# Two transformer layers on one core: the activation tile H, and all that is allocated behind it, 32 bytes further on in SBUF

## The chip, the cores and the metric

The kernel runs on one core of one Trainium2 chip. The time is device microseconds (us) of one execution. Three executions of the kernel before took 2331.41, 2332.02 and 2332.15 us; the median is 2332.02 us.

## What is computed

A sequence of 256 tokens with 2048 features, all in float32, goes through two layers. Layer 0 mixes tokens with gated linear attention, layer 1 with grouped-query attention. Both have the same MLP and the same gated embedding behind it. Cut to what matters here:

```python
for i in range(2):
    u = rms_norm(h, g_pre_mix[i])
    mix = gla_mixer(u, ...) if i == 0 else gqa_mixer(u, ...)        # both end with  o @ w_out
    h = h + rms_norm(mix, g_post_mix[i])
    hid = relu(rms_norm(h, g_pre_mlp[i]) @ w_mlp_up[i])              # [256, 2048] @ [2048, 8192]
    h = h + rms_norm((hid * hid) @ w_mlp_down[i], g_post_mlp[i])     # [256, 8192] @ [8192, 2048]
    gate = sigmoid(h @ w_ple_gate[i])                                # [256, 2048] @ [2048, 2048]
    h = h + rms_norm(gate * (p[i] @ w_ple_proj[i]), g_ple[i])
```

## The kernel before

**Three products for one.** Each float32 operand is split into a high and a low float32r part, and a product is made of three matmuls: high by high, high by low, low by high. Weights come by DMA in chunks of two contraction tiles by 512 columns (`raw`, 4 buffers), and ScalarE and VectorE split each into `whi` and `wlo` (4 buffers each, lines 91 and 92). An activation tile holds both parts beside each other: `X` and `H` are each 128 partitions by 16 contraction tiles by 512, where the first 256 elements of a contraction tile are the high part of the 256 tokens and the other 256 the low part.

**Two kinds of product.** `gemm_b` (lines 367 and 372) makes a transposed result: the weights are loaded into the array (they are the stationary operand, 128x128) and the activations stream through (the moving operand). A pair of its matmuls streams 512 and then 256 columns. `gemm_a` (lines 294 to 296) makes a result by rows: the activations are stationary and 512 columns of the weights stream. `gemm_out` (lines 333 to 335) is a `gemm_a` whose last 512 columns are made one row tile after the other, and for them half of the weights wait in the activation tile that is free at that time (`keep`). So in the gate's product `g` some matmuls stream weights out of `H` while `X` is stationary, and in the last down product `d` some stream weights out of `X` while `H` is stationary. The second row tile of these columns is made in two parts of 256 columns. In the profile a matmul is written out<-moving,stationary: `d<-whi,H` streams `whi` against a stationary piece of `H`.

**The order.** The stages follow one another on TensorE, in an order that is written out: q, k, v, then the output gate `og` and the output product `go` of layer 0; four times an up product `u` of 2048 columns (from `X` into `H`) and a down product `d` (from `H`); the gate product `g`; then in layer 1 `kp`, `vp`, `q`, the attention, the output product `ao`, and again four times `u` and `d`, and `g`. `H` is the stationary operand of `go`, `ao` and `d`; `X` that of `v`, `kp`, `vp`, `q` and `g`.

**Where the tiles lie.** Tile pools are laid out one behind the other, and every tile starts at a multiple of 32 bytes of each partition. By the built program `X` starts at byte 33,824, the `raw` buffers at 66,592 and every 4,096 bytes on, `whi` at 82,976 and `wlo` at 99,360 and every 4,096 bytes on: all of them 32 modulo 64. Their places also agree modulo 512, 1024 and 2048. `H` is the first tile of the pool `L1` (line 804) and starts at byte 171,968, which is 0 modulo 64. Matmul operands are pieces of 512, 1024 or 2048 bytes at multiples of 512 bytes within their tile, so each piece has its tile's place modulo 64. Behind `H` lie the other tiles of `L1` (the helpers `t1` and `t2` of the up product, `PT`, the gain rows, the low parts of keys and values `kvlow`) and, last, the attention's small pool `att`.

Of the kernel before, what the change touches and what calls it, by code (L numbers as in the profile page):

```python
# [10 lines left out]
F32 = mybir.dt.float32  # L11
# [6 lines left out]
P = 128  # L18
# [37 lines left out]


class WeightStream:
    """Weight chunks in the order of use: DMA in, split exactly into two float32r parts."""

    def __init__(self, nc, pool, nraw, nsplit):
        self.nc, self.pool, self.nraw, self.nsplit = nc, pool, nraw, nsplit
# [29 lines left out]
        self.todo.append(lambda: self.nc.vector.tensor_sub(lo, raw, hi.bitcast(F32)))  # L92

    def parts(self, i):
        """The first chunk comes one contraction tile at a time, so that PE starts early."""
        kt = self.chunks[i][1]
        return [(k, k + 1) for k in range(kt)] if i == 0 else [(0, kt)]

# [52 lines left out]
def kernel(ctx, tc, a, out):  # L151
# [9 lines left out]
    def acc(name):  # L161
        return psa.tile([P, 512], F32, tag="acc", name=name)
# [79 lines left out]
    def rstd_of(ss, dim, name):  # L242
        n = ss.shape[1]
        ms = sm.tile([P, 2], F32, tag="ms", name=name + "_ms")[:, :n]
        nc.vector.tensor_reduce(ms, ss, axis=AX.X, op=ALU.add)
        nc.vector.tensor_scalar(ms, ms, 1.0 / dim, EPS, op0=ALU.mult, op1=ALU.add)
        r = sm.tile([P, 2], F32, tag="rstd", name=name, bufs=3)[:, :n]
        nc.gpsimd.tensor_tensor(r, ms, mhalf[:, :n], op=ALU.pow)
        return r
# [24 lines left out]
    def region_open():  # L274
        region.enter_context(tc.manual_schedule(engines={mybir.EngineType.Activation, mybir.EngineType.DVE}))

    def gemm_a(op, ngroups, evac, nk=16, name="a", pair=False):
        nch = nk // KC
        order = [(g, c) for g in range(ngroups) for c in range(nch)]
        if pair:  # L280
            order = pair_order(nch) + [(g, c) for g in range(2, ngroups) for c in range(nch)]
        ps = {}
        for g, c in order:
            if c == 0:
                ps[g] = [acc(f"{name}_{g}_{t}") for t in range(NT)]
            hi, lo = W.get()
            seq = [(k, t) for k in range(KC) for t in range(NT)]
            if c == nch - 1:
                seq = [(k, t) for t in range(NT) for k in range(KC)]
            for k, t in seq:  # L290
                K = c * KC + k
                xh = op[:, K, t * P:(t + 1) * P]
                xl = op[:, K, T + t * P:T + (t + 1) * P]
                mm(ps[g][t], xh, hi[:, k], start=K == 0, stop=False)  # L294
                mm(ps[g][t], xh, lo[:, k], start=False, stop=False)  # L295
                mm(ps[g][t], xl, hi[:, k], start=False, stop=K == nk - 1)  # L296
                if K == nk - 1:
                    evac(g, t, ps[g][t])
            yield (g, c)

    def gemm_out(op, keep, evac, name, pair=False):
        """Four column groups; the last one row tile after the other, half of its weights waiting in `keep`."""
        nch = KT // KC
        p0 = W.pos + 3 * nch
        for c in range(NSPLIT):
            W.dest[p0 + c] = [keep[:, 4 * c + 2 * z:4 * c + 2 * z + 2].rearrange("p k n -> p (k n)") for z in range(2)]
        yield from gemm_a(op, 3, evac, name=name, pair=pair)
        for t in range(NT):
            parts = [(0, 512)] if t == 0 else [(0, 256), (256, 256)]
            ps = [acc(f"{name}_3_{t}_{o}") for o, _ in parts]  # L310
            order = [[c] for c in range(nch)]
            if t:
                order = order[NSPLIT:] + order[:NSPLIT]
                order[-2:] = [order[-2] + order[-1]]
            for n, cs in enumerate(order):
                end = n == len(order) - 1
                if t and end:
                    region_open()
                wt = {}
                for c in cs:  # L320
                    W.ahead()
                    wt[c] = W.pop(p0 + c) if t else W.split[p0 + c]
                if t and end:
                    W.pos += nch
                for (o, w), p_ in zip(parts, ps):
                    s = slice(o, o + w)
                    ck = [(c, k) for c in cs for k in range(KC)]
                    for c, k in ck:
                        K = c * KC + k
                        hi, lo = wt[c]  # L330
                        xh = op[:, K, t * P:(t + 1) * P]
                        xl = op[:, K, T + t * P:T + (t + 1) * P]
                        mm(p_[:, :w], xh, hi[:, k, s], start=n == 0 and k == 0, stop=False)
                        mm(p_[:, :w], xh, lo[:, k, s], start=False, stop=False)
                        mm(p_[:, :w], xl, hi[:, k, s], start=False, stop=end and (c, k) == ck[-1])
                    if end:
                        evac(3, t, p_[:, :w], o, w)
                yield (3, cs[0])
# [8 lines left out]
        return r  # L347

    def early(m, ss, name):
        """The update of the residual's first rows, while PE is at the second."""  # L350
        r = rstd_of(ss[:, :1, :4], D, name)
        for n in range(4):
            residual_n(m, r, n, (0,))
# [84 lines left out]
                                           op0=ALU.mult, op1=ALU.add)  # L438

    def boundary(m, ss, gain0, name, fill=(), late=None):  # L440
        """The normalised update of the residual and the next operand; fill: products that keep PE busy."""
        rstd = last_rstd(ss, name)
        mults = list(pend)
        pend.clear()
        W.ahead(1, lows=False)
        for f in fill[:-1]:
            f()()
        for o in (0, 256):
            nc.vector.scalar_tensor_tensor(h[:, 1, o:o + 256], m(1, 0)[:, o:o + 256], rstd, h[:, 1, o:o + 256],
                                           op0=ALU.mult, op1=ALU.add)  # L450
        W.lows()
        make_X(0, gain0)
        if late is not None:
            late(0)
        if fill:
            fill[-1]()()
        residual_n(m, rstd, 1, (1,))
        W.ahead(1)

        def hook(n):  # L460
            def f():
                make_X(n, gain0)
                if n == 2:
                    for g in mults:
                        g()
                if n < 3:
                    residual_n(m, rstd, n + 1, (1,))
                if late is not None:
                    late(n)
                if n == 3:  # L470
                    region.close()
            return f
        hooks = {0: [hook(1)], 2: [hook(2)], 4: [hook(3)]}
        if late is not None:
            at(hooks, 6, lambda: late(4))
        return hooks
# [137 lines left out]
    with tc.tile_pool(name="core", bufs=1) as cp:  # L614
# [150 lines left out]
        s = fold(ps, "lr", 32)  # L765
# [35 lines left out]
        sl = drive(gemm_a(X, 4, v_evac, name="v"), plan, sl)  # L801

    L1 = ctx.enter_context(tc.tile_pool(name="L1", bufs=1))
    H = L1.tile([P, KT, 512], F32R, name="H")

    def load_PT(i):
        pts = L1.tile([P, 2, T], F32, tag="pts", name=f"pts{i}")
        nc.scalar.dma_start(pts, a["pT"][i])
        PT = L1.tile([P, 2, 512], F32R, tag="PT", name=f"PT{i}")
        split_into(PT[:, :, :T], PT[:, :, T:], pts)  # L810
        return PT

    def og_evac(i, ps):
        s = fold(ps, f"og{i}")
        t1 = L1.tile([P, T], F32, tag="t1", name=f"og1_{i}", bufs=2)
        nc.vector.tensor_mul(t1, s, R0["r"])
        sg = L1.tile([P, T], F32, tag="t2", name=f"og2_{i}", bufs=2)
        nc.scalar.activation(sg, t1, AF.Sigmoid)
        nc.vector.tensor_mul(t1, t1, on[i // 4][:, i % 4])
        nc.vector.tensor_mul(t1, t1, sg)  # L820
        split_into(H[:, i, :T], H[:, i, T:], t1)
    drive(gemm_b(X, 4, og_evac, name="og"), plan, sl)
# [3 lines left out]
    mg = {}  # L826
    gr = gain_row(L1, a["g_post_mix"][0], "gpm0")
    ss = sm.tile([P, NT, 5], F32, tag="ss", name="ssm0")
    drive(gemm_out(H, X, out_evac(mg, gr, ss, "go"), "go"))

    RM = {}
# [13 lines left out]
    def mlp_ple(i, hooks, PT):  # L845
# [5 lines left out]
        def up_evac(f, ps):  # L851
# [3 lines left out]
            nc.scalar.activation(s2, s, AF.Square)  # L855
            split_into(H[:, f, :T], H[:, f, T:], s2)

# [16 lines left out]
        for q in range(4):  # L874
# [3 lines left out]
            if q < 3:  # L878
                drive(gemm_a(H, 4, down_evac(q), name=f"d{q}"))
            else:  # L880
                drive(gemm_out(H, X, down_evac(q), f"d{q}"))
        hooks = boundary(lambda t, n: macc[t][n], ss, None, f"rpl{i}", eprojs(e, range(EU[0] if i == 0 else EU[2], 8), PT))
# [24 lines left out]
        def upd(t, n):  # L907
            return e[n][:, t]
        drive(gemm_out(X, H, gate_evac, f"g{i}"), hooks)
        return upd, ss2  # L910

# [265 lines left out]
```

## Time and profile before

| | us |
|---|---|
| median of three executions | 2332.02 |
| lowest and highest | 2331.41, 2332.15 |
| span of the profiled execution | 2329.9 |
| TensorE busy in the span | 2305.6 |
| VectorE busy | 1423.1 |
| ScalarE busy | 1213.8 |

The span runs from the first instruction to the last; 2.1 us of the median lie around it. Matmuls overlap in the pipeline: a row's duration (0.39 us for 512 columns) is longer than the distance to the next row's start, and it is the distance that adds up to the span. So paces are read from start times here: the start of one row, the start of a later one, and the count of matmuls between them.

### The profile page before, as it was taken

How to read it: one execution, taken by the hardware profiler on the slowest of the kernel's cores; microseconds unless marked ns; L12 is line 12 of the kernel's file. 1: busy time of each engine (PE TensorE's matmuls, PEld its weight loads, DVE VectorE, ACT ScalarE, POOL GpSimd, SP SyncE). 2: the span in 40 equal slices, each digit the busy share in tenths (PEclk: the TensorE clock that was granted, in tenths of full speed). 3: DMA queues.
4: the chain of work that ended last, by engine and by line, in shares of the span. 5: the costliest groups of instructions: out<-in, count | busy, mean ns of one | idle time of the engine just before them, and what ended most of it. 6: DMA issues, size and time to landing. Idle time of an engine off the chain costs nothing.

```text
span 2329.9 us, 31200 instructions
## 1 busy us (share of the span) xinstructions
PE 2305.6 (99%) x11924; PEld 1955.4 (84%) x11924; DVE 1423.1 (61%) x1920; ACT 1213.8 (52%) x1884; POOL 36.7 (2%) x58
## 2 busy tenths in 40 slices
PE   8989999999999999999999999999999999999998
PEld 7878888988888888888888888888888888888887
DVE  6787765664564565556667676665455455455565
ACT  6666554654453454454456565555454355355454
POOL 0000000000000000000000010000000000000000
PEclk9999999999999999999999999999999999999999
DMA  8544665665665665665565644565565566566654
GB/s 285 158 145 144 203 187 189 192 188 189 189 190 186 187 188 186 188 191 187 194 216 160 181 137 158 200 190 189 186 187 189 187 189 189 187 187 188 210 171 145
DMA packets 223784, 431.75 MB, mean 185 GB/s; under 512 B 15697, under 2 KB 16721, under 8 KB 222865
## 3 DMA queue, kind: packets, MB, share of 16 engines
q1 hardware_dynamic: 221328, 421.23, 58.7%
q10 hardware_dynamic: 2304, 8.52, 1.0%
q8 instruction: 93, 1.52, 0.3%
q14 instruction: 59, 0.48, 0.1%
HBM read 427.60 MB, written 2.10 MB: 184 GB/s over the span
## 4 chain that ended last, share of the span: by engine, by line
PE 96%; DVE 1%; ACT 1%; issue 1%; DMA 0%; POOL 0%; SPq 0%; DVEq 0%; POOLq 0%; ACTq 0%
PE u L367 20%; PE u L372 10%; PE d L296 10%; PE d L294 10%; PE d L295 10%; PE og L367 3%; PE g L295 2%; PE g L294 2%; PE g L296 2%; PE og L372 1%; PE q L294 1%; PE q L296 1%; PE q L295 1%; PE k L367 1%; PE go L296 1%; PE ao L295 1%
## 5 line engine op out<-in xcount | busy, mean ns | idle before, releaser
L92 DVE TENSOR_TENSOR wlo<-raw,whi 128x1024 fp32r<-128x1024 f32 (+1 forms) x770 | 937.6, 1221 | 751.4 <-ACT whi L91 749.1
L91 ACT CAST whi<-raw 128x1024 fp32r<-128x1024 f32 (+1 forms) x770 | 805.5, 1049 | 875.3 <-PE d L296 357.3
L367 PE MATMUL u<-X,whi 128*128 128x512 f32 x2048 | 716.7, 395 | 0.0
L372 PE MATMUL u<-X,wlo 128*128 128x256 f32 x2048 | 572.1, 280 | 0.0
L367 PEld LDWEIGHTS u<-X,whi 128*128 128x128 f32 x2048 | 383.8, 187 | 89.5
L372 PEld LDWEIGHTS u<-X,wlo 128*128 128x128 f32 x2048 | 386.1, 189 | 0.4
L296 PE MATMUL d<-whi,H 128*128 128x512 f32 x960 | 380.6, 396 | 0.0
L294 PE MATMUL d<-whi,H 128*128 128x512 f32 x960 | 379.7, 395 | 0.0
L295 PE MATMUL d<-wlo,H 128*128 128x512 f32 x960 | 377.3, 393 | 0.0
L295 PEld LDWEIGHTS d<-wlo,H 128*128 128x128 f32 x960 | 180.2, 188 | 44.5
L296 PEld LDWEIGHTS d<-whi,H 128*128 128x128 f32 x960 | 180.2, 188 | 43.9
L294 PEld LDWEIGHTS d<-whi,H 128*128 128x128 f32 x960 | 180.2, 188 | 42.5
L367 PE MATMUL og<-X,whi 128*128 128x512 f32 x256 | 89.4, 393 | 0.0
L294 PE MATMUL g<-whi,X 128*128 128x512 f32 x192 | 75.2, 392 | 0.0
L295 PE MATMUL g<-wlo,X 128*128 128x512 f32 x192 | 74.7, 389 | 0.0
L296 PE MATMUL g<-whi,X 128*128 128x512 f32 x192 | 74.7, 389 | 0.0
L372 PE MATMUL og<-X,wlo 128*128 128x256 f32 x256 | 71.7, 280 | 0.0
L367 PEld LDWEIGHTS og<-X,whi 128*128 128x128 f32 x256 | 47.9, 187 | 10.5
L409 ACT COPY u_c<-u 128x256 f32<-128x256 f32 x128 | 47.1, 368 | 17.1 <-PE u L372 17.1
L367 PE MATMUL q<-X,whi 128*128 128x512 f32 x128 | 46.2, 411 | 6.1 <-ACT whi L91 5.3
L295 PE MATMUL v<-wlo,X 128*128 128x512 f32 x128 | 50.7, 396 | 0.8 <-DVE wlo L92 0.8
L294 PE MATMUL v<-whi,X 128*128 128x512 f32 x128 | 51.5, 402 | 0.0
(426 smaller groups left out, 2978.4 us busy)
## 6 DMA issues: line engine op xcount, KB each, us to landing
raw<-in_w_mlp_up SPq DMA_DIRECT2D x256, 512.0 KB, 3.7
raw<-in_w_mlp_down SPq DMA_DIRECT2D x256, 512.0 KB, 3.8
raw<-in_gla_w_in SPq DMA_DIRECT2D x95, 512.0 KB, 4.0
raw<-in_w_ple_gate SPq DMA_DIRECT2D x64, 512.0 KB, 4.2
raw<-in_attn_w_in SPq DMA_DIRECT2D x48, 512.0 KB, 4.2
raw<-in_gla_w_out SPq DMA_DIRECT2D x32, 512.0 KB, 4.3
raw<-in_attn_w_out SPq DMA_DIRECT2D x32, 512.0 KB, 4.3
raw<-in_w_ple_proj SPq DMA_DIRECT2D x7, 512.0 KB, 5.2
```

What stands on the lines that cost most here:

```text
L91: self.nc.scalar.copy(hi, raw)
L92: self.todo.append(lambda: self.nc.vector.tensor_sub(lo, raw, hi.bitcast(F32)))
L294: mm(ps[g][t], xh, hi[:, k], start=K == 0, stop=False)
L295: mm(ps[g][t], xh, lo[:, k], start=False, stop=False)
L296: mm(ps[g][t], xl, hi[:, k], start=False, stop=K == nk - 1)
L367: mm(ps[f], hi[:, k, f * P:(f + 1) * P], op[:, K, :], start=K == 0, stop=K == 15, skip_group_check=True)
L372: mm(ps[f][:, T:], lo[:, k, f * P:(f + 1) * P], op[:, K, :T], start=False, stop=K == 15, skip_group_check=True)
L409: nc.scalar.copy(cr[:parts], ps[:parts, T:])
```

## The change

One line allocates a tile of 8 float32 (32 bytes) ahead of `H`, which nothing reads or writes. `H` then starts at byte 172,000, and every tile of `L1` and `att` lies 32 bytes further on too, so that they go from 0 to 32 modulo 64. `H` now has the place of `X` and of the weight buffers modulo 64, but not modulo 128 (96 against 32). No other tile moves. The list of instructions of each engine, their order and the semaphores that they wait for are the same in both programs. Three docstrings become empty lines; the code below line 803 has line numbers greater by one.

```diff
     L1 = ctx.enter_context(tc.tile_pool(name="L1", bufs=1))
+    L1.tile([P, 8], F32, name="gap")
     H = L1.tile([P, KT, 512], F32R, name="H")
```

## Rows read from the trace of the kernel before

**Rows 1.** The page: span, TensorE's busy time, engines of the chain that ended last

```profile
span 2329.9 us, 31200 instructions
PE 2305.6 (99%) x11924; PEld 1955.4 (84%) x11924; DVE 1423.1 (61%) x1920; ACT 1213.8 (52%) x1884; POOL 36.7 (2%) x58
PE 96%; DVE 1%; ACT 1%; issue 1%; DMA 0%; POOL 0%; SPq 0%; DVEq 0%; POOLq 0%; ACTq 0%
```

**Rows 2.** TensorE's timeline, second down product: start us, us, engine, line, out<-moving,stationary

```profile
700.14 0.39 PE L294 MATMUL d<-whi,H 128*128 128x512 f32 x1
...
770.14 0.39 PE L294 MATMUL d<-whi,H 128*128 128x512 f32 x1
```

**Rows 3.** The same view in the first gate product

```profile
1170.28 0.39 PE L296 MATMUL g<-whi,X 128*128 128x512 f32 x1
...
1210.39 0.39 PE L296 MATMUL g<-whi,X 128*128 128x512 f32 x1
```

**Rows 4.** The same view at the end of that gate product

```profile
1214.02 0.40 PE L333 MATMUL g<-H,X 128*128 128x512 f32 x1
...
1219.64 0.40 PE L333 MATMUL g<-whi,X 128*128 128x512 f32 x1
...
1225.09 0.28 PE L333 MATMUL g<-whi,X 128*128 128x256 f32 x1
...
1230.84 0.28 PE L333 MATMUL g<-H,X 128*128 128x256 f32 x1
...
1236.47 0.28 PE L517 MATMUL e<-whi,PT 128*128 128x256 f32 x1
```

**Rows 5.** The same view at the end of the last down product

```profile
2203.14 0.40 PE L333 MATMUL d<-X,H 128*128 128x512 f32 x1
...
2208.74 0.40 PE L333 MATMUL d<-whi,H 128*128 128x512 f32 x1
...
2214.34 0.28 PE L333 MATMUL d<-whi,H 128*128 128x256 f32 x1
```

**Rows 6.** Groups by line and shape on TensorE: count | busy us, mean ns | idle before

```profile
L294 PE MATMUL d<-whi,H 128*128 128x512 f32 x960 | 379.7, 395 | 0.0
L294 PE MATMUL go<-whi,H 128*128 128x512 f32 x96 | 37.6, 392 | 0.0
L294 PE MATMUL ao<-whi,H 128*128 128x512 f32 x96 | 38.2, 398 | 0.0
L517 PE MATMUL e<-whi,PT 128*128 128x256 f32 x64 | 18.6, 290 | 0.0
L333 PE MATMUL g<-H,X 128*128 128x512 f32 x16 | 6.3, 397 | 0.0
L333 PE MATMUL d<-X,H 128*128 128x512 f32 x16 | 6.3, 396 | 0.0
L333 PE MATMUL go<-X,H 128*128 128x512 f32 x8 | 3.1, 392 | 0.0
```

**Rows 7.** TensorE's timeline where two up products of layer 0 begin and end

```profile
602.29 0.40 PE L367 MATMUL u<-X,whi 128*128 128x512 f32 x1
...
691.04 0.39 PE L294 MATMUL d<-whi,H 128*128 128x512 f32 x1
...
780.63 0.40 PE L367 MATMUL u<-X,whi 128*128 128x512 f32 x1
...
871.08 0.40 PE L294 MATMUL d<-whi,H 128*128 128x512 f32 x1
```

**Rows 8.** Busy time by stretch, second down and first gate product: PE, PEld, DVE, ACT, POOL, PEclk, DMA, GB/s

```profile
700.00:770.00 70.00, 70.00 (x302) 56.31 (x301) 34.21 (x31) 26.18 (x26) 0.00 (x0) 1.00 0.59 188
1170.00:1210.00 40.00, 40.00 (x178) 33.10 (x178) 24.54 (x25) 21.63 (x28) 0.00 (x0) 1.00 0.62 207
```

**Rows 9.** Groups on VectorE, of equal shape: out in H, out in a tile that stays

```profile
L237 DVE TENSOR_TENSOR H<-sq,H 128x256 fp32r<-128x256 f32 x128 | 49.0, 420 | 0.0
L410 DVE TENSOR_TENSOR u_s<-u,u_c 128x256 f32<-128x256 f32 x128 | 48.1, 417 | 0.0
```

## The prediction, made before the changed kernel ran

> **What bounds the kernel now.** I read the page first. TensorE is busy for 2305.6 of 2329.9 us and makes 96% of the chain that ended last [rows 1], so only its pace can move the time by much. The change leaves every instruction, its order and its waits as they are; what can change is how long a matmul takes whose operand lies elsewhere. So the second view is TensorE's timeline, by start times, for matmuls of one shape with operands in different places.
>
> In the second down product, 300 matmuls of 512 columns start from 700.14 to 770.14 us [rows 2]: 70.00 / 300 = 233.3 ns each. In the gate product 177 start from 1170.28 to 1210.39 [rows 3]: 40.11 / 177 = 226.6 ns. Shape, clock (granted 1.00 in both, so 2.4 GHz) and instruction are equal, and no matmul waits [rows 6, 8]. What differs is that d holds a piece of H (0 modulo 64 bytes) while weights at 32 stream, and g holds a piece of X (32) while weights at 32 stream.
>
> The end of the gate product tells whether that is the stage or the place. There 24 matmuls stream weights that were parked in H against X, and the next 24 stream `whi` against the same X. The first run takes 1219.64 - 1214.02 = 5.62 us, or 234.2 ns each; the second 1225.09 - 1219.64 = 5.45 us, or 227.1 ns [rows 4]. In the same stage, on the same stationary tile, the pace turns with the buffer that streams. The reverse stands at the end of the last down product: H is stationary there, first X and then `whi` stream, both at 32, and 24 matmuls take 5.60 us each time (2203.14, 2208.74, 2214.34 [rows 5]): 233.3 ns, no turn. So neither "H stationary" nor "H moving" is slow by itself: a pair at 32 and 32 runs at 226.7, a pair at 0 and 32 at 233.3, whichever operand is at 0.
>
> The size of the step fits a 64-byte grain. At 32 and 32, 48 matmuls of 256 columns take 1230.84 - 1225.09 = 5.75 us, 119.8 ns each [rows 4]; 256 more columns cost 226.7 - 119.8 = 106.9 ns, or 0.417 ns a column: one cycle of 2.4 GHz. The step between the two paces, 6.67 ns, is then 16 columns, which are 64 bytes of float32. That is an inference, not a shown mechanism.
>
> **The change part by part.**
>
> *Matmuls of 512 columns that touch H.* d has three lines of 960, thus 2,880, and in its last columns six groups of 16 (three stream weights, three stream X), 96. go has 3 x 96 and six groups of 8, together 336; ao the same, 336. The gate products stream H in three groups of 16, 48. Of each kind one group stands in [rows 6]. Sum: 3,696. All turn from 0 and 32 into 32 and 32. If they then run as g does: 3,696 x (233.33 - 226.67 ns) = **-24.6 us**. All of it is on the chain: these lines have no idle time ahead of them [rows 6]. ao runs partly among attention matmuls; I take the same step there, and if none came it would be 336 x 6.67 = 2.2 us less.
>
> *What must keep up.* In d a weight chunk is used up in 12 matmuls, 2.80 us now, 2.72 us then. VectorE is busy for 34.21 of 70 us there and ScalarE for 26.18; in the gate product, at the faster pace, VectorE is at 24.54 and ScalarE at 21.63 of 40 us and the DMA at 207 GB/s against 188 [rows 8], and TensorE does not wait. So the cover holds, with the gate product as the proof.
>
> *Matmuls of 256 columns that touch H.* With X stationary and H streaming, 48 take 1236.47 - 1230.84 = 5.63 us, 117.3 ns; at 32 and 32 it is 119.8. Two such runs, 96 x 2.5 ns: **+0.2 us**. Those of d stand near 120 on either side: nothing.
>
> *PT and the rest of L1.* PT is stationary in three groups of 64 products with 256 columns [rows 6]. By the same 2.5 ns it is at most 192 x 2.5 = 0.5 us either way; I take 0. VectorE takes 420 ns for a result in H and 417 for the same shape into a tile that does not move [rows 9], so I take 0 for ScalarE's and VectorE's work there too; it lies beside TensorE's anyway.
>
> *The up products.* They don't touch H on TensorE, but they have two paces. The second takes 691.04 - 602.29 = 88.75 us, the third 871.08 - 780.63 = 90.45 us [rows 7], for the same 256 pairs of matmuls: 346.7 against 353.3 ns a pair. The operands are the same and at 32 and 32 both times, so here the pace is a state that the stage enters with and keeps. At 346.7 ns the pair is what the gate's paces add up to (226.7 + 119.8); at 353.3 it is one step of 6.67 ns more. Of the six up products that follow a down product, three are in either state, in turn, which is what a train of matmuls with a cycle would hand on. 256 x 6.67 ns = 1.7 us a stage. If the down products run in step, all six enter alike: all fast is 3 x 1.7 = -5.1 us, all slow is +5.1 us. No row shows an up product entered from an undisturbed train at 32 and 32. I take fast, because the fast pair is the sum of the two paces at equal places, and the slow one needs an odd offset at the start. The two up products that follow a boundary between stages can turn as well, 1.7 us each, one either way; I take 0.
>
> *Sum.* -24.6 + 0.2 - 5.1 = -29.5 us. On the span: 2329.9 - 29.5 = 2300.4; with the 2.1 us around it, against the median of 2332.02, **2302.5 us**.
>
> **The rivals.**
>
> *In step, but the up products slow.* -24.6 + 0.2 + 5.1 = -19.3 us: 2312.7 us. For it: half of the stages are in that state now. Against it: the reason above.
>
> *Nothing changes.* X and the weight buffers agree not only modulo 64 but modulo 2048, and all matmuls of rows 3 have operands that agree modulo 512. H's new place agrees modulo 64 alone. If the grain is 128 bytes or more, the pair stays out of step and the time is 2332.0 us. Only the size of the step, 16 columns, speaks for 64. The Trainium skill has two statements by which nothing would change either. "TensorE: Matmul & The Clock Gate", section "Step-by-step: what each phase is for", says that the moving operand and the weight load have read ports of their own and that loading the next weights takes nothing from the running matmul; "SBUF — State Buffer", section "Specifications (TRN2)", gives lines of 16 bytes, and both of H's places begin one. By either rule the time would be 2332.0 us; the trace disagrees already, with 234.2 and 227.1 ns in one stage [rows 4].
>
> *Slower.* What counts is the distance between the operands, in steps, and not whether they agree modulo 64. Then 32 bytes more of distance may cost a step more instead of one less: 3,696 x 6.67 = +24.6 us, 2356.6 us. It decides if the matmuls that touch H go to 240 ns. Against it: H streaming against X and X streaming against H have the opposite sign of distance and the same pace [rows 4, 5].
>
> **How the numbers follow.** In step and up products fast: 0.50, 2302.5 us. In step and up products slow, or a mixture: 0.31, up to 2312.7 us. Nothing changes: 0.13, 2332.0 us. Slower: 0.06, 2356.6 us. The range must hold the first two with their open ends: below, the first up product of layer 0 fast too and PT's 0.5 us, 2302.5 - 1.7 - 0.5 = 2300.3; above, slow up products, one more of them (1.7), no gain in ao (2.2) and PT (0.5), 2312.7 + 4.4 = 2317.1. I give 2299 to 2318; it leaves out the last two cases, 0.19. A measurement here tells about 0.2% (4.7 us) from no change; both cases in step are beyond it, so faster 0.81, same 0.13, slower 0.06.
>
> **What would show it.** In the trace of the changed kernel: `d<-whi,H` 226.7 ns apart and a down product of 384 matmuls in 87.0 us instead of 89.6; in the gate product no turn between the run that streams H and the run that streams `whi`; up products of 88.75 us each where they follow a down product (90.45 is the first rival). If d stays at 233.3 ns, the grain is not 64 bytes and the prediction is wrong in its main term; if d turns and the time falls by much less than 19 us, something else has begun to wait, to be seen as idle time ahead of lines 294 to 296.

## The result, and the profile after

The changed kernel takes 2317.93 us (four executions, 2316.52 to 2318.60) against 2332.09 us for the kernel before in the same session (2331.41 to 2334.52). The ratio is 0.9936, with a 95% interval of 0.9922 to 0.9950. So it is faster, by 14.2 us or 0.6%, about half of the gain that was forecast: the forecast of 2302.5 us was 15.4 us too low. The time lies 0.07 us inside the range that was given, and 0.8 us above the 2317.1 us that the prediction worked out for its upper end.

The page of the changed kernel, answering to [rows 1]: the span, the busy time of the engines, and the engines of the chain that ended last.

```profile
span 2315.6 us, 31200 instructions
PE 2290.2 (99%) x11924; PEld 1953.4 (84%) x11924; DVE 1423.6 (61%) x1920; ACT 1214.0 (52%) x1884; POOL 36.6 (2%) x58
PE 95%; DVE 2%; ACT 1%; issue 1%; POOL 0%; DMA 0%; SPq 0%; DVEq 0%; POOLq 0%; ACTq 0%
```

The span is 14.3 us shorter than before, and TensorE's busy time 15.4 us. VectorE and ScalarE have the same work in the same time, and the chain is TensorE's as it was. The chain shows nothing new that waits, so the place to look at is again TensorE's pace, the distance between starts.

TensorE's timeline in the second down product, answering to [rows 2] (start us, us, engine, line, out<-moving,stationary), and below it the busy time of that stretch (PE, PEld, DVE, ACT, POOL, granted clock, DMA share, GB/s), answering to [rows 8].

```profile
700.22 0.39 PE L296 MATMUL d<-whi,H 128*128 128x512 f32 x1
...
768.89 0.39 PE L296 MATMUL d<-whi,H 128*128 128x512 f32 x1
```

```profile
700.00:768.00 68.00, 68.00 (x299) 55.80 (x298) 34.02 (x31) 26.32 (x25) 0.00 (x0) 1.00 0.60 190
```

300 matmuls take 68.67 us: **228.9 ns** each, at the same full clock, where they took 233.3 before and 226.7 were forecast. That is neither of the two paces that [rows 2, 3] show. From single starts it is a cycle of three: the starts are 226, 229 and 232 ns apart in turn, and nine matmuls take 2.06 us, which is 9 x 226.67 plus three steps of 6.67 ns.

The end of the gate product, answering to [rows 4]: 24 matmuls stream `H`, 24 stream `whi` with 512 columns, 48 with 256 columns.

```profile
1207.75 0.39 PE L333 MATMUL g<-H,X 128*128 128x512 f32 x1
...
1213.35 0.39 PE L333 MATMUL g<-whi,X 128*128 128x512 f32 x1
...
1218.81 0.28 PE L333 MATMUL g<-whi,X 128*128 128x256 f32 x1
...
1224.56 0.29 PE L333 MATMUL g<-H,X 128*128 128x256 f32 x1
...
1230.02 0.28 PE L517 MATMUL e<-whi,PT 128*128 128x256 f32 x1
```

The turn is still there: 5.60 / 24 = 233.3 ns with `H` streaming, 5.46 / 24 = 227.5 with `whi`. The same two tiles that in the down product (H stationary) came to 228.9 stay at 233.3 when their parts are exchanged. So the pace depends on which operand lies further on, not only on whether they agree. The last 48, of 256 columns with `H` streaming, come to 113.7 ns (1230.02 - 1224.56 = 5.46 us), where they took 117.3 before [rows 4].

The end of the last down product, answering to [rows 5].

```profile
2189.87 0.39 PE L333 MATMUL d<-X,H 128*128 128x512 f32 x1
...
2195.37 0.39 PE L333 MATMUL d<-whi,H 128*128 128x512 f32 x1
...
2200.86 0.28 PE L333 MATMUL d<-whi,H 128*128 128x256 f32 x1
...
2206.30 0.28 PE L333 MATMUL d<-X,H 128*128 128x256 f32 x1
```

24 matmuls of 512 columns take 5.50 and 5.49 us, 229 ns, and 48 of 256 columns 5.44 us, 113.3 ns. Before, these took 120.0 (2220.10 - 2214.34 = 5.76 us, from [rows 5] and this line of the same view of the kernel before):

```profile
2220.10 0.28 PE L333 MATMUL d<-X,H 128*128 128x256 f32 x1
```

The up products, answering to [rows 7].

```profile
598.34 0.39 PE L367 MATMUL u<-X,whi 128*128 128x512 f32 x1
...
688.78 0.39 PE L294 MATMUL d<-whi,H 128*128 128x512 f32 x1
...
776.67 0.40 PE L367 MATMUL u<-X,whi 128*128 128x512 f32 x1
...
867.12 0.39 PE L294 MATMUL d<-whi,H 128*128 128x512 f32 x1
```

The second takes 90.44 us (688.78 - 598.34) and the third 90.45, with a down product of 87.89 between them. Of the six up products behind a down product five now have the slow pace, 353.3 ns a pair, where three had it.

Stage by stage, by the first starts on TensorE, in us:

| | before | after | difference |
|---|---|---|---|
| six down products of 384 matmuls | 6 x 89.6 | 6 x 87.9 | -10.2 |
| two last down products | 96.60, 94.78 | 94.24, 92.65 | -4.5 |
| `go`, `ao` | 96.60, 106.04 | 94.81, 104.43 | -3.4 |
| eight up products | 723.12 | 726.54 | +3.4 |
| first product q | 26.20 | 27.47 | +1.3 |
| all else | | | -0.9 |
| span | 2329.9 | 2315.6 | -14.3 |

The first q runs before `H` is used. In the kernels below it took anything from 25.6 to 28.3 us, so its 1.3 us belong to the start of an execution and are no result of the change.

### The profile page after: what moved, and what is told of

The parts are those of the page before. It is cut to its first block, busy times and chain, and to the rows that moved or that the text cites. A ratio compares the mean times of both kernels' runs of the same rounds, so it can differ in the third digit from the quotient of the medians.

```text
span 2315.6 us, 31200 instructions
## 1 busy us (share of the span) xinstructions
PE 2290.2 (99%) x11924; PEld 1953.4 (84%) x11924; DVE 1423.6 (61%) x1920; ACT 1214.0 (52%) x1884; POOL 36.6 (2%) x58
## 4 chain that ended last, share of the span: by engine, by line
PE 95%; DVE 2%; ACT 1%; issue 1%; POOL 0%; DMA 0%; SPq 0%; DVEq 0%; POOLq 0%; ACTq 0%
PE u L367 21%; PE u L372 10%; PE d L295 10%; PE d L296 10%; PE d L294 9%; PE og L367 3%; PE g L296 2%; PE g L294 2%; PE g L295 2%; PE og L372 1%; PE q L296 1%; PE q L295 1%; PE q L294 1%; PE k L367 1%; PE go L295 1%; PE ao L296 1%
## 5 line engine op out<-in xcount | busy, mean ns | idle before, releaser
L296 PE MATMUL d<-whi,H 128*128 128x512 f32 x960 | 376.5, 392 | 0.0
L294 PE MATMUL d<-whi,H 128*128 128x512 f32 x960 | 374.3, 390 | 0.0
```

## Experiments

### Is it a grain, and of how many bytes?

Three kernels differ from the changed one only in the size of the unused tile: 24, 16 or 32 float32 in place of 8.

```diff
-    L1.tile([P, 8], F32, name="gap")
+    L1.tile([P, 24], F32, name="gap")
```

With 24, `H` starts at byte 172,064 and agrees with `whi` and `X` modulo 256, 512 and 1024.

> The gap ahead of H is 96 bytes instead of 32: H starts at byte 172,064 and agrees with X and the weight buffers modulo 64, 128, 256, 512 and 1024. Theory 'distance' (the pace of a 512-column matmul goes by the distance between its stationary and its moving piece, modulo more than 64 bytes): d, go and ao at 226.7 ns, as g, and in the last columns of the gate product no turn between the run that streams H and the one that streams whi. Theory 'place of the stationary piece' (by its own place modulo 128): also 226.7 ns for d, but the run of g that streams H, whose stationary piece has always been in X, cannot have been slow by it. If the grain were 64 bytes after all and something else held d at 228.9 ns: 228.9 ns as with 32 bytes. Time, if d is in step: 2332.1 - 24.6 = 2307.5 us with the up products as before; 2302.7 if the six that follow a down product are all fast, 2312.9 if all are slow. The 256-column matmuls of d, which went from 120 to 113.3 ns with the 32 bytes, go back to 120.

TensorE's timeline in the second up and second down product of this kernel:

```profile
598.97 0.39 PE L367 MATMUL u<-X,whi 128*128 128x512 f32 x1
...
689.41 0.40 PE L294 MATMUL d<-whi,H 128*128 128x512 f32 x1
...
700.09 0.39 PE L296 MATMUL d<-whi,H 128*128 128x512 f32 x1
...
768.09 0.39 PE L296 MATMUL d<-whi,H 128*128 128x512 f32 x1
```

300 matmuls take 68.00 us: 226.7 ns, the pace that was forecast. The down products take 87.1 us, and in the gate product the turn is gone (24 matmuls `g<-H,X` at 226.7). But the up product takes 90.44 us, and so do all six behind a down product. The 256-column matmuls of `d` are back at 120, as expected. The kernel takes 2316.15 us against 2333.98 beside it, ratio 0.9931 (0.9917 to 0.9944): not clear of the changed kernel. That is 3.3 us more than was expected with all six slow; the kernel before ran 1.9 us higher beside it than it had beside the changed kernel. Of the 5.4 us that the stages with H stationary gain over that one, the eight up products, now all slow, hand back 3.0. Another 1.7 us go in the stretch from k to v, which runs before `H` is used.

With 16, `H` starts at 172,032, and with 32 at 172,096; both are 0 modulo 64, as before.

> The gap is 64 bytes: H starts at 172,032, which is 0 modulo 64, as before the change, and 480 bytes (-32) from the weight buffers modulo 512. A 64-byte grain: d at 233.3 ns and the time of before, 2332 us. Distance modulo more than 64: a pace between 226.7 and 233.3 ns that need not be that of before.

> The gap is 128 bytes: H starts at 172,096. Modulo 128 it lies where it lay before the change (64), modulo 512 it does not (64 against 448), and its distance from the weight buffers is 32 modulo 512 (416 before). If the pace goes by anything modulo 128, d is back at 233.3 ns and 256-column matmuls of d at 120 ns, and the time is about 2332 us; if the modulus is larger, d has another pace.

The second down product with 16:

```profile
699.80 0.39 PE L294 MATMUL d<-whi,H 128*128 128x512 f32 x1
...
769.80 0.39 PE L294 MATMUL d<-whi,H 128*128 128x512 f32 x1
```

70.00 us for 300, 233.3 ns, and the same with 32 (700.13 to 770.13). The times are 2336.83 and 2335.79 us, ratios 1.0014 (1.0003 to 1.0024) and 1.0008 (0.9997 to 1.0018): no gain, and up products that are all slow with 16 and mostly slow with 32. So there are three paces for the same instruction, and which one holds goes by H's place: 0 bytes from the weights modulo 256 gives 226.7 ns, 192 gives 228.9, and 32, 160 and 224 give 233.3.

### The whole table of distances

A probe that leaves out both layers (its outputs are copies of the last train's sums) issues trains of 24 matmuls of 512 columns, of 256 columns, and of the two in turn, and moves the stationary piece by 32 bytes from train to train. The trains of 512 columns run for four places of the moving piece. A line and the end of the call are cut here.

```diff
+    def train(name, m, s, widths):
...
+        ps = psa.tile([P, 512], F32, tag="acc", name=name, bufs=8)
+        for n in range(N):
+            w = widths[n % len(widths)]
+            o = 8 * s + 128 * (n % 4)
+            mm(ps[:, :w], S[:, o:o + P], M[:, 8 * m:8 * m + w], ...)
```

> Not the layer: it leaves out all of the computation and runs trains of 24 matmuls on copies of x, alone on the chip, with nothing on ScalarE and VectorE beside them. The stationary piece starts s x 32 bytes into its tile (s = 0 to 31), the moving piece m x 32 bytes into its own (m = 0 to 3; both tiles agree modulo 512); trains of 512 columns for each m and s, of 256 columns and of alternating 512 and 256 columns for m = 0. 'Distance': the time of a train goes by s - m alone, 24 x 226.7 = 5.44 us at 0 and at 16 x 32 = 512 bytes if the modulus is 512 or less, 24 x 228.9 = 5.49 us at -64 bytes, 5.60 us at -96 bytes. 'Place of the stationary piece': it goes by s and not by m. If the pace in the layer comes from ScalarE's and VectorE's traffic beside the matmuls, all trains take the same time.

The timeline of the probe, grouped by train. The last letter is the stationary piece's place in steps of 32 bytes (a is 0), the one before it the moving piece's (w is 0, x is 1). What counts is the distance between starts of rows; a train's first matmul still belongs to the entry.

```profile
21.64 5.61 PE L45 MATMUL fullwa<-M,S 128*128 128x512 f32 x24
27.09 5.75 PE L45 MATMUL fullwb<-M,S 128*128 128x512 f32 x24
32.68 5.76 PE L45 MATMUL fullwc<-M,S 128*128 128x512 f32 x24
...
49.49 5.76 PE L45 MATMUL fullwf<-M,S 128*128 128x512 f32 x24
55.09 5.67 PE L45 MATMUL fullwg<-M,S 128*128 128x512 f32 x24
60.60 5.76 PE L45 MATMUL fullwh<-M,S 128*128 128x512 f32 x24
66.19 5.61 PE L45 MATMUL fullwi<-M,S 128*128 128x512 f32 x24
...
199.85 5.77 PE L45 MATMUL fullxa<-M,S 128*128 128x512 f32 x24
205.45 5.64 PE L45 MATMUL fullxb<-M,S 128*128 128x512 f32 x24
210.93 5.75 PE L45 MATMUL fullxc<-M,S 128*128 128x512 f32 x24
```

From a to b it is 5.45 us, the five trains from b to g take 5.59 to 5.61 each (28.00 together), g 5.51, h 5.59, and with i, 256 bytes on, the row begins again. With the moving piece one step on, the short train is xb: it is the distance of the two, stationary less moving, that counts. By the starts within each train, without the entry:

| stationary less moving, modulo 256 bytes | 0 | 32 | 64 | 96 | 128 | 160 | 192 | 224 |
|---|---|---|---|---|---|---|---|---|
| 512 columns, ns each | 226.7 | 233.3 | 233.3 | 234.2 | 233.3 | 233.3 | 228.9 | 233.3 |
| 256 columns, ns each | 120.0 | 118.2 | 117.8 | 117.3 | 118.7 | 120.0 | 117.8 | 117.8 |

This repeats four times over 1,024 bytes, for 512 columns at each of the four places of the moving piece and for 256 columns at the one place that was run. Nothing ran on VectorE or ScalarE beside the trains, so these paces don't come from memory traffic of theirs.

The table gives every 512-column pace of the layers: `d` before is at distance 160 (233.3), after at 192 (228.9), with 24 float32 at 0 (226.7), with 16 at 224 and with 32 at 32 (both 233.3). The gate's `g<-H,X` has the distance the other way round, 96 before (234.2 in [rows 4]) and 64 after (233.3).

For 256 columns it agrees only in part. Groups at distance 0 run at 120 in the layers too, and `go` and `ao` in the changed kernel (192) at 117.8, but `d` in the same kernel, at the same 192, runs at 113.3. The `go` of the changed kernel:

```profile
400.48 0.28 PE L333 MATMUL go<-whi,H 128*128 128x256 f32 x1
...
406.13 0.28 PE L333 MATMUL go<-X,H 128*128 128x256 f32 x1
```

48 matmuls take 5.65 us, 117.7 ns. The gate's `g<-H,X` at 64 (113.7 against 117.8 in the trains) and `go` and `d` with 16 float32 at 224 (116.7 against 117.8) differ from the trains as well. So the distance alone doesn't set the pace of a 256-column matmul. What else does is open.

### What sets an up product's pace

The pairs of an up product (512 and 256 columns) are at distance 0 in all the kernels so far and still have two paces. A second probe, which leaves out both layers as well, runs a lead train, in some cases a few matmuls between, and then 24 pairs.

```diff
+    def case(i, lead, between, pairs):
+        train(f"lead{word(i)}", lead)
+        if between:
+            train(f"then{word(i)}", between)
+        return train(f"pair{word(i)}", pairs)
```

> Again trains of matmuls on copies of x and nothing of the layer; it leaves out all of the computation. The question is the up product's two paces. Each case is a lead train of 512-column matmuls, in some cases a few matmuls of another width or distance, and then 24 pairs of 512 and 256 columns, most at distance 0. 'State' (at distance 0 a train of pairs holds the pace that it enters with): 24 pairs take either 24 x 346.7 = 8.32 us or 24 x 353.3 = 8.48 us, and which of them goes by what stands ahead: by the length of a lead train at distance 160 or 192 bytes, and by the inserted matmuls. At distances 96 and 224 bytes, where the trains of e4_trains always took 346.7 ns, it should be 8.32 us whatever stands ahead. 'Memory traffic': the two paces come from ScalarE's and VectorE's work beside the up product; then all cases here at distance 0 are alike.

The timeline of this probe, grouped by train (`lead`, what stands between as `then`, and the pairs):

```profile
28.47 8.63 PE L43 MATMUL paira<-M,S 128*128 128x512 f32 x48
36.95 5.61 PE L43 MATMUL leadb<-M,S 128*128 128x512 f32 x24
...
104.03 0.33 PE L43 MATMUL thenf<-M,S 128*128 128x128 f32 x2
104.20 8.54 PE L43 MATMUL pairf<-M,S 128*128 128x512 f32 x48
112.57 5.62 PE L43 MATMUL leadg<-M,S 128*128 128x512 f32 x24
...
273.95 8.63 PE L43 MATMUL pairr<-M,S 128*128 128x512 f32 x48
282.43 6.13 PE L43 MATMUL leads<-M,S 128*128 128x512 f32 x26
288.39 8.48 PE L43 MATMUL pairs<-M,S 128*128 128x512 f32 x48
296.72 6.34 PE L43 MATMUL leadt<-M,S 128*128 128x512 f32 x27
...
434.89 8.48 PE L43 MATMUL pairC<-M,S 128*128 128x512 f32 x48
443.22 5.76 PE L43 MATMUL leadD<-M,S 128*128 128x512 f32 x24
```

Entered straight from a train at distance 0 (a), 24 pairs take 8.48 us, 353.3 ns each. With two matmuls of 128 columns between (f) they take 8.37, entry included, and behind one matmul of 512 columns at distance 32 or 192 they are fast too (8.32). One of 128 columns, one at 96, or any number of 256 columns at distance 0 that was tried leaves them slow. Behind a train at distance 192 they are slow after 24, 25, 27, 28, 30 and 31 matmuls (r is 25) and fast after 26, 29 and 32 (s is 26: 8.33 us, 347 ns), the cycle of three again. Behind a train at 160 they are fast. Pairs at a distance of 96 or 224 (C) are fast from each of the three entries tried. So at distance 0 the pair has two paces, each of which keeps itself up, and the last matmuls ahead choose between them. Nothing on VectorE or ScalarE is needed for it. A down product has 384 matmuls, a multiple of three, so in the changed kernel the probe says slow, as five of six are (the sixth it doesn't explain); with `H` at distance 0 it says slow for all, as the first experiment shows.

### Three ways to turn the up products

All three start from the kernel with 24 float32 (`H` at distance 0). The first only issues the first chunk's matmuls in another order, eight of 512 columns and then eight of 256:

```diff
-            drive(gemm_b(X, 4, up_evac, name=f"u{q}", fresh=q == 0), hooks if q == 0 else None)
+            drive(gemm_b(X, 4, up_evac, name=f"u{q}", fresh=True), hooks if q == 0 else None)
```

> The gap of 96 bytes, and all up products, not only the first of each layer, begin with 8 matmuls of 512 columns, then 8 of 256, before they go on in pairs. 'State': an up product may enter otherwise than in e1_h96, where nearly all were slow; if the six after a down product go fast, 6 x 1.7 = 10 us less than e1_h96, about 2306 us; if the entry does not matter or the state falls the same way, 2316 us as e1_h96. 'Memory traffic': no change, 2316 us.

The second up product of this kernel:

```profile
598.63 1.98 PE L367 MATMUL u<-X,whi 128*128 128x512 f32 x8
...
689.03 0.40 PE L294 MATMUL d<-whi,H 128*128 128x512 f32 x1
```

2315.62 us, ratio 0.9925 (0.9909 to 0.9942) to the kernel before; every up product behind a down product still takes 90.40 us. The probe's like case, 8 and 8 at distance 0, is slow as well.

The second places another 56 float32 behind `X`, so that all that follows, the weights and `H` with them, lies 224 bytes from `X` modulo 256, where the probe's pairs were always fast:

```diff
+    base.tile([P, 56], F32, name="gapx")
```

> The gap of 96 bytes ahead of H, and 224 bytes between X and the weight buffers, so that all behind X moves by 224: weights and X are now 224 bytes apart modulo 256, H and the weights still 0. 'Distance modulo 256': d, go and ao stay at 226.7 ns; all 1,632 matmuls of 512 columns that hold X and stream weights or H go to 233.3 ns (32 modulo 256), +10.9 us at most; the up products are all at 346.7 ns, as 224 bytes showed in e4_trains, 2048 x 6.6 = -13.5 us against e1_h96; together about 2313 us. If places modulo 64 or 128 counted, X at 32 against weights at 0 would be slow for up products too.

The second up product and a stretch of the gate product of this kernel (its lines are greater by one):

```profile
596.33 0.40 PE L368 MATMUL u<-X,whi 128*128 128x512 f32 x1
...
685.10 0.39 PE L295 MATMUL d<-whi,H 128*128 128x512 f32 x1
...
1170.20 0.40 PE L295 MATMUL g<-whi,X 128*128 128x512 f32 x1
...
1210.80 0.40 PE L334 MATMUL g<-whi,X 128*128 128x512 f32 x1
```

All six take 88.76 or 88.77 us, and the two ahead of them 91.88, the shortest of any kernel. The price stands in the gate: 174 matmuls in 40.60 us, 233.3 ns, because with X stationary the distance is now 32. The gates are 2.0 us longer each, the second layer's q 1.6, v 0.8. The sum: 2308.73 us, ratio 0.9895 (0.9881 to 0.9910). The expectation of about 2313 us was too high: the stages with X stationary cost 7.4 us in place of up to 10.9, and the stretch from k to v, whose pairs are at 224 now too, took 2.2 us less than with 24 float32 alone.

The third leaves the places alone and issues two small matmuls ahead of each up product, whose result the next matmul overwrites:

```diff
+                if name[0] == "u" and c == 0 and g == fresh:
+                    for _ in range(2):
+                        mm(ps[0][:, :P], hi[:, 0, :P], op[:, 0, :P], start=True, stop=True, skip_group_check=True)
```

> The gap of 96 bytes, and two more matmuls of 128 columns at the start of each up product (of the two that follow a boundary, at the start of their second group, behind the transposes). Their result is overwritten by the matmul that follows. In e5_entries two such matmuls between a lead train at distance 0 and the pairs turned the pairs from 353.3 to 346.7 ns. 'State': the six up products after a down product take 88.8 us instead of the 90.5 of e1_h96, and so three quarters of the other two if a slow train can be turned too: 2316.2 - 6 x 1.7 - 2 x 1.3 = 2303.4 us, or 2306 if only the six turn. If the state in the layer is set otherwise than on the bare trains: 2316 us plus 8 x 0.17 us for the added matmuls.

The timeline at the second up product of this kernel, the two small matmuls first:

```profile
599.01 0.33 PE L376 MATMUL u<-X,whi 128*128 128x128 f32 x2
599.18 0.45 PE L367 MATMUL u<-X,whi 128*128 128x512 f32 x1
...
687.98 0.40 PE L294 MATMUL d<-whi,H 128*128 128x512 f32 x1
```

From 599.01 to 687.98 us: 88.97, with the two small ones in it, against 90.44 without them. All six are so. The up products at a stage's beginning stay slow (93.69 and 93.70 us), where the two matmuls stand one column group later, inside a train that is slow already. The kernel takes 2307.13 us (2306.10 to 2307.44), ratio 0.9888 (0.9872 to 0.9903). That is the lowest of this study, though its interval and that of the kernel before this one overlap, and some 11 us less than the changed kernel, by the two ratios.

### The small matmuls without the move

> The kernel before, with no gap (H at distance 160 from the weights), and the same two matmuls of 128 columns in each up product. d stays at 233.3 ns. In e5_entries a lead train at distance 160 left the pairs fast by itself, with nothing inserted, so the inserted ones may as well turn them slow: all six alike, 5.1 us faster or slower than the median of before, with the six alternating as before only if the two matmuls change nothing.

The third up product of this kernel, which took 90.45 us before:

```profile
780.44 0.33 PE L376 MATMUL u<-X,whi 128*128 128x128 f32 x2
...
869.41 0.39 PE L294 MATMUL d<-whi,H 128*128 128x512 f32 x1
```

The same two matmuls in the kernel before: all six up products take 88.97 us (three of them took 90.44), `d` stays at 233.3 ns (89.60 us a product), and the second layer's first up product turned slow (93.58 from 92.07). 2331.55 us against 2332.92, ratio 0.9992 (0.9983 to 1.0001): too small to be told from no change.

So the two parts can be set apart. The down products go by the place of H and not by the small matmuls. The six up products take the same 88.97 us at either place of H once the small matmuls stand ahead of them; without these the place of H reaches them through the train that leads in. Their worth can be read apart too: with H at distance 0 the stages that hold H stationary are 23.5 us shorter than before, and the small matmuls take 3.7 us off the six up products of the kernel before, and 8.8 us where all six were slow.

## Why the prediction was wrong in size and right in sign

**The time inside the range: luck.** The upper end of the range was worked out from matmuls on H that gain in full, up products that are slow, and small losses beside them. What came was a smaller gain on H and up products that are mostly slow. The two together ended 0.07 us below the upper end, and two of the four executions lie above it.

**That the distance between starts is what the change moves, and nothing else: right.** No new wait in the chain, the other engines unchanged, and the cover in the down product held at the faster pace. The guess at nothing for VectorE's and ScalarE's work in H agrees with their busy times within 0.5 us.

**The grain of 64 bytes: the step that failed.** From one pace at "32 and 32" and one at "0 and 32" the prediction made a rule of agreement modulo 64, on the ground that the step of 6.67 ns is 16 columns, which are 64 bytes. The trains show the period to be 256 bytes, the value at 0 to be the only one at 226.7, and a third pace of 228.9 at 192, where the change put H. So the two paces of before were samples from a table of eight entries, and neither is that of the new place. The working itself held the warning: X and the weights agree modulo 2048, so that any grain up to that fitted [rows 3], and only an argument from a like number (16 columns, 64 bytes) chose the smallest. There was also a small sign against two paces: the 234.2 and 233.3 ns of [rows 4, 5] are 96 and 160 bytes, and the trains keep them apart, while the text took them as one.

**The term of -24.6 us: mis-sized.** It priced 3,696 matmuls at 6.67 ns. 3,648 of them, with H stationary, gained 4.44 ns each, which makes -16.2; the 48 that stream H gained hardly anything. Some 1.7 us more came from matmuls of 256 columns, which the prediction had at nothing (96 in each last down product went from 120.0 to 113.3 ns: 0.6 us each; those of `go` and `ao` from 120 to 117.8: 0.2 us each). The 96 in the gates that stream H, priced at +0.2 us, went from 117.3 to 113.7 ns, which is -0.3. Together the stages with H stationary gave -18.1 us. That the term was right for a place truly in step is shown by the kernel with H at distance 0: `d` at 226.7 ns and 87.1 us, as written.

**The up products: wrong in sign.** -5.1 us were taken and the eight gave +3.4. The reason given, that the fast pair is the sum of the two paces and a slow one needs an odd offset at the start, is refuted: a train at distance 0 leads into the slow pace (353.3 ns, case a). The first rival said that they could all be slow, and with H at distance 0 they all are. In the changed kernel it was five of six. The sentence that the pace is a state which the stage enters with and keeps was right, and could be shown by two small matmuls that turn it.

**The rivals.** In the up products the kernel came out near the first rival (+3.4 us where that had +5.1), but not in H: -18.1 us where it had -24.6, and so 2317.9 in place of 2312.7. "Nothing changes" named the right doubt, a grain of 128 bytes or more; it did not happen, because the step is not all or nothing. The slower rival had half of the mechanism: it is the distance of the operands, with its sign, that counts. Its argument against itself, equal paces for both signs, compared 96 with 160, which only happen to lie close. The two statements of the Trainium skill that were cited ("TensorE: Matmul & The Clock Gate", section "Step-by-step: what each phase is for"; "SBUF — State Buffer", section "Specifications (TRN2)") would have given no change. The runs do not agree with that result: 226.7 to 234.2 ns for one instruction, by the distance between its two operands alone, in trains that did nothing else.

**The sum.** Of the 15.2 us between -29.5 and -14.3, 6.2 are the stages with H stationary, 8.5 the up products, and the remaining half a microsecond the first q against small gains elsewhere.

**What stays open.** What in the chip has a period of 256 bytes is not shown; only that it is one. Why the up products of the kernel before alternated is not settled: the trains at 160 left the pairs fast for 24, 25 and 26 matmuls, yet three of six were slow there. Each kernel has one trace, and the pace of pairs can differ where kernels are alike: the first pairs of k, issued before `H` is used and with all their operands in the same places, ran at 346.7 ns in the changed kernel and at 353.3 with 24 float32. So it is not shown that the up products split in the same way in every execution. The 113.3 ns of `d`'s 256-column matmuls is open, as said. And the tiles behind H moved with it in every kernel here; what they contribute alone was not tried, though the stages between q and `ao` in the second layer, which use them, changed by 0.5 us at most in the kernels that left X in its place with the weights.

## What to carry to other kernels

Where a kernel is bound by matmuls that load new weights each time, read the paces of one shape from start to start, and compare the two operands' places modulo 256 bytes: here equal places were worth 3% of a 512-column matmul at distance 160, at the cost of one unused tile, but they also let the pairs of the up products run slow. A pace read at two places is two samples, not a rule; before a period is inferred from it, a train over all places is one short kernel. Where matmuls of two sizes alternate, the pace can also be a state handed on from the train ahead, and two small matmuls made a stage of 90.4 us 1.5 us shorter, their own 0.2 us counted.

## What the runs showed of the hardware that was not expected

The time of a float32r matmul with a weight load of its own depends on the distance from moving to stationary operand, modulo 256 bytes: 226.7 ns at 0, 228.9 at 192, 234.2 at 96, 233.3 elsewhere, for 512 columns; at 256 columns distance 0 is among the slowest of the trains (120.0 against 117.3 at 96), and in the layers one distance (192) had two paces, 117.8 and 113.3. At 192 the pace is a cycle of three matmuls, and what follows depends on the count modulo three. Pairs of 512 and 256 columns at distance 0 have two paces that keep themselves up, 346.7 and 353.3 ns, and which one holds is chosen by the last matmuls ahead.
